# Expert 0's first rows built on TensorE from fp32 row tiles, with the experts' ranking and the splitting of weights in another order

## The chip, the cores and the metric

One core of a Trainium2 chip runs the whole block in one launch. The metric is the device time of one execution in microseconds (us), as the median of several runs. Engines are named as the profile names them: PE is TensorE's matrix product, PEld its weight load, DVE VectorE, ACT ScalarE, POOL GpSimd, SP the queue that issues most transfers.

## The reference

```python
hn = rms_norm(h, attn_norm_g[l])
u_raw, v_raw, q, k, v, gate_a, gate_b = split(hn @ w_in[l])
a = gmlp_chunk_mixer(u_raw, v_raw, ...)
b = swa_sink_attention(q, k, v, sinks, rel_bias)
merged = sigmoid(gate_a) * (a @ w_proj_a[l]) + sigmoid(gate_b) * (b @ w_proj_b[l])
h = h + merged @ w_out[l]
hn = rms_norm(h, ffn_norm_g[l])
# hierarchical MoE on hn: the best of 4 groups, in it the best 2 of 4 experts
for e in range(16):
    hid = silu(t @ w_gate[e]) * (t @ w_up[e])
    out = out + combine[:, e:e + 1] * (hid @ w_down[e])
h = h + out
return rms_norm(h, final_norm_g)
```

All is float32: 1024 tokens of 1024 channels, 16 experts with 512 hidden channels. A token goes to two experts, so an expert has about 128 tokens, some more and some fewer.

## The kernel before

Every large product is made of three fp32r products of a high part and a low part (`mm3`, lines 198 to 201): ACT writes the high part (a copy to fp32r), DVE subtracts it from the source and writes the low part. For weights this is done in "granules" of 128 x 1024 (`Granules`, from line 247): `high(g)` is an ACT instruction (line 299), `low(g)` a DVE instruction (line 305 for the gate and up weights, line 309 for the down weights), and `load_others(g)` then lets SP load a later granule into the raw buffer that became free. Expert e has the granules 12e to 12e+11: eight of gate and up (k = 0 to 7), four of down. In the tables of the change "h3" and "l3" are the high and the low part of granule 3 of the next expert.

The first part (norms, mixers, output projection) works on two halves of four 128-token tiles. In the second half the four tiles 4 to 7 leave the output projection one by one. For each `logits` makes the router's products and `route` chooses the experts, counts ranks within each expert on PE, and scatters the normalised rows (`row`, 1024 channels and a few words more) into the queues `xs_d` in DRAM by two indirect transfers on POOL. From the last tile on, DVE and ACT run in the order in which the code is written, and in the experts all engines do.

Expert 0 must begin while the rows of the last tiles are still on their way to `xs_d`. So its first 128 rows are put together in the core: the rows of tiles 0 to 5 are read back from `xs_d` into `early` (a DMA of POOL, line 1051), and the rows of tiles 6 and 7 (`LATE`) are placed by PE (`place`, line 1038): a 128 x 128 matrix of ones and zeros (`oh`, "place" in the profile) times the row tile, whose high and low parts (`hl`) come from ACT and POOL (line 1078). The sum lies in PSUM as rows; DVE adds it to `early` (line 1238), PE transposes the sum (eight transposes, `transpose_x`, line 1325), and ACT and DVE split it into `xT`. Then PE loads expert 0's count of tokens into a register, and branches: over 128 tokens it computes a second tile of the expert (`last_tile`), else it goes on. In the shown execution expert 0 has no second tile.

`order_experts` sorts the other experts by their counts (first part: ranks and row offsets; second part: counts and tables) in small DVE instructions, and writes them into `ints`. PE, ACT, DVE, POOL and SP read their branch conditions from there. The order of all this inside an expert's tile is set by `ahead(step)`: after a step such as ("f1", 7) or ("y", 1) of the matrix products it runs what the tables `AHEAD_0`, `AHEAD_1` and `AHEAD` name. `fill(k)` makes the expert's first two steps beside the second tile of the expert, with `FIRST` = 3 granules of the next expert in `fill(0)`.

## Time and profile before

| | us |
|---|---|
| median of 3 runs | 1094.59 |
| the three runs | 1091.77, 1094.59, 1094.70 |
| profiled execution | 1091.46 |
| its span | 1089.7 |
| PE busy in the span | 1023.1 (94%) |
| DVE busy | 724.8 (67%) |
| ACT busy | 608.7 (56%) |
| POOL busy | 107.6 (10%) |

The span runs from the first to the last profiled instruction; 1.8 us of the execution lie around it. In the profile a row of the timeline gives the start in us from the span's start, the time until the last instruction of the row ended, engine and line, what is written and read, how many instructions, and in brackets how long the engine had been idle and what ended that. Matrix products overlap: one of 512 columns is shown with 0.39 us, but they start 0.23 us after each other. A row with windows gives the busy time of each engine in a stretch, the granted clock of TensorE as a share of full speed, and the share of the DMA engines.

### The profile page before, as it was taken

The numbers are of one execution on the slowest core, as the hardware profiler recorded it, in microseconds if no ns is written. First come the engines' busy times: TensorE is split into PE (matmuls) and PEld (weight loads), VectorE is DVE, ScalarE is ACT, GpSimd is POOL, SyncE is SP. The second block draws the span as 40 slices with busy tenths as digits, with TensorE's granted clock in tenths as the row PEclk, the third lists the DMA queues.
The fourth block names the chain that finished last, engine by engine and source line by source line (L and its number), as shares of the span: only waits on it lengthen the run. The fifth ranks groups of instructions, "written<-read, shape, count | busy, mean of one in ns | idle before, by whom it ended". The sixth has DMA issues, their size and how long they took to land. (4 is left out here: it accounts for less than half of the span.)

```text
span 1089.7 us, 15458 instructions
## 1 busy us (share of the span) xinstructions
PE 1023.1 (94%) x4775; PEld 821.1 (75%) x4775; DVE 724.8 (67%) x1584; ACT 608.7 (56%) x1016; POOL 107.6 (10%) x132
## 2 busy tenths in 40 slices
PE   7999899999999999999999958899999999999893
PEld 6778788788888888887888846677777777777682
DVE  6852577675368555776445788978769686848735
ACT  5543465543356464555335447676858686847743
POOL 4001000000004000000001041111111112010020
PEclk9999999999999999999999989999999999999997
DMA  8432545645137413222646546969898989979854
GB/s 248 122 106 102 173 157 166 188 140 184 44 120 273 140 54 97 83 72 68 203 152 215 196 175 223 330 241 319 281 334 258 313 293 285 306 240 309 252 218 191
DMA packets 125478, 214.47 MB, mean 197 GB/s; under 512 B 11563, under 2 KB 58731, under 8 KB 125360
## 3 DMA queue, kind: packets, MB, share of 16 engines
q1 hardware_dynamic: 112016, 176.58, 48.6%
q0 software_dynamic: 7200, 21.20, 7.0%
q10 hardware_dynamic: 6144, 15.27, 3.8%
q8 instruction: 56, 0.92, 0.3%
q14 instruction: 62, 0.51, 0.1%
HBM read 185.46 MB, written 37.63 MB: 205 GB/s over the span
## 5 line engine op out<-in xcount | busy, mean ns | idle before, releaser
L305 DVE SCALAR_TENSOR_TENSOR w_e<-raw_e,g2T,w_e 128x1024 fp32r<-128x1024 f32 x127 | 156.1, 1280 | 22.9 <-ACT w_e L299 16.6
L299 ACT ACTIVATE w_e<-raw_e,g2T 128x1024 fp32r<-128x1024 f32 x127 | 137.5, 1142 | 15.1 <-DMA raw_e<-in_expert_w_up_dram 4.5
L199 PE MATMUL ps_gu<-w_e,xT 128*128 128x512 f32 x256 | 104.2, 407 | 8.9 <-ACT w_e L299 4.1
L201 PE MATMUL ps_gu<-w_e,xT 128*128 128x512 f32 x256 | 101.8, 398 | 1.1 <-DVE xT L177 1.1
L1413 PE MATMUL ps_y<-w_e,hT 128*128 128x512 f32 x384 | 100.4, 404 | 1.1 <-DVE hT L177 0.9
L200 PE MATMUL ps_gu<-w_e,xT 128*128 128x512 f32 x256 | 101.5, 396 | 0.0
L1413 PEld LDWEIGHTS ps_y<-w_e,hT 128*128 128x128 f32 x384 | 69.9, 190 | 17.3 <-DVE hT L177 1.8
L309 DVE TENSOR_TENSOR w_e<-raw_e,w_e 128x1024 fp32r<-128x1024 f32 x63 | 75.0, 1218 | 0.8 <-ACT w_e L299 0.8
L299 ACT ACTIVATE w_e<-raw_e 128x1024 fp32r<-128x1024 f32 x63 | 65.7, 1054 | 0.4 <-DMA raw_e<-in_expert_w_down_dram 0.2
L199 PEld LDWEIGHTS ps_gu<-w_e,xT 128*128 128x128 f32 x256 | 48.7, 190 | 20.7 <-issue 9.7
L201 PEld LDWEIGHTS ps_gu<-w_e,xT 128*128 128x128 f32 x256 | 48.8, 190 | 12.9 <-DVE xT L177 1.5
L200 PEld LDWEIGHTS ps_gu<-w_e,xT 128*128 128x128 f32 x256 | 48.8, 191 | 10.1
L201 PE MATMUL ps_o<-w_wo,ms 128*128 128x512 f32 x128 | 51.3, 402 | 0.0
L200 PE MATMUL ps_o<-w_wo,ms 128*128 128x512 f32 x128 | 51.1, 400 | 0.0
L199 PE MATMUL ps_o<-w_wo,ms 128*128 128x512 f32 x128 | 51.1, 399 | 0.0
L199 PE MATMUL ps_ga<-xh,w_ga 128*128 128x512 f32 x128 | 50.8, 397 | 0.0
L200 PE MATMUL ps_ga<-xh,w_ga 128*128 128x512 f32 x128 | 50.7, 396 | 0.0
L201 PE MATMUL ps_ga<-xh,w_ga 128*128 128x512 f32 x128 | 50.6, 396 | 0.0
L200 PE MATMUL ps_gb<-xh,w_gb 128*128 128x512 f32 x128 | 50.6, 395 | 0.0
L201 PE MATMUL ps_gb<-xh,w_gb 128*128 128x512 f32 x128 | 50.6, 395 | 0.0
L199 PE MATMUL ps_gb<-xh,w_gb 128*128 128x512 f32 x128 | 50.6, 395 | 0.0
L567 PE MATMUL ps_gv<-w_gv,xh 128*128 128x512 f32 x192 | 46.9, 397 | 3.9 <-ACT xh L176 2.5
(540 smaller groups left out, 2379.8 us busy)
## 6 DMA issues: line engine op xcount, KB each, us to landing
raw_e<-in_expert_w_gate_dram SPq DMA_DIRECT2D x127, 256.0 KB
raw_e<-in_expert_w_up_dram SPq DMA_DIRECT2D x127, 256.0 KB
raw_e<-in_expert_w_down_dram SPq DMA_DIRECT2D x63, 512.0 KB
xs_d<-zero ACTq DMA_DIRECT2D x16, 516.0 KB
xt_last<-xs_d SPq DMA_DIRECT2D x32, 258.0 KB
raw_ga<-in_w_in_dram SPq DMA_DIRECT2D x16, 512.0 KB
raw_gb<-in_w_in_dram SPq DMA_DIRECT2D x16, 512.0 KB
raw_wo<-in_w_out_dram SPq DMA_DIRECT2D x16, 512.0 KB
```

Of the source, the lines that this page charges most:

```text
L199: nc.tensor.matmul(acc, lhi, rhi, start=start, stop=False)
L200: nc.tensor.matmul(acc, lhi, rlo, start=False, stop=False)
L201: return nc.tensor.matmul(acc, llo, rhi, start=False, stop=stop)
L299: nc.scalar.activation(self.split_tiles[g][:, 0, :], self.raw[g], AF.Copy, **scale)
L305: nc.vector.scalar_tensor_tensor(w[:, 1, :], raw, g2T[:, k : k + 1], w[:, 0, :], ALU.mult, ALU.subtract)
L309: nc.vector.tensor_tensor(w[:, 1, :], raw, w[:, 0, :], ALU.subtract)
L567: nc.tensor.matmul(accs[i], xh[a][k // 4][:, k % 4, t], gs[j][:, b, k % 2, :], start=k + a + b == 0, stop=k == KT - 1 and b == 1,)
L1413: nc.tensor.matmul(ys[nh], hT[:, a, k, :], dn[k][:, b, nh * 512 : (nh + 1) * 512], start=k + i == 0, stop=k == FK - 1 and i == 2,)
```

## The change

- `LATE` takes in tile 5, so `early` holds tiles 0 to 4 and is read back before the scatters of tile 5.
- `place` no longer takes a high and a low part. The row tile is the stationary operand and the 128 x 128 one-hot matrix streams past it, both in plain fp32, in eight products of 128 columns for the eight blocks of channels. The result is already transposed. `early` is added in the same way with the identity as the one-hot matrix, as the last eight products. The `hl` tiles, ACT's and POOL's instructions for them, DVE's two additions and the eight transposes go.
- Tile 5's products stand around the transposes of tile 7's `logits`; tile 6's behind the logits; tile 7's and `early`'s at the end.
- High parts of granules 9, 10, 11 and 12 are issued on ACT within tile 7's routing; 20 warming transposes there become 10, and the 32 at the program's start become 42.
- Count and tables of expert 0 come ahead of `transpose_x`, the first part of `order_experts` right behind it, and the second part after ("y", 2) of expert 0 ahead of that step's low parts. Low parts of the next experts move to later steps (`AHEAD_0`, `AHEAD_1`), expert 1's `fill(0)` splits none, and one comparison (`at`) is made twice.
- Expert 0 has one form of a second tile left (a whole one), so it has one branch and less code in between.

```diff
-LATE = (6, 7)
+LATE = (5, 6, 7)
-AHEAD_0 = {("f1", 7): "h3 l3 h4 l4", ("y", 0): "h5 l5 h6 l6 h7 l7", ("y", 1): "h8 l8 h9 l9 h10 l10 h11 l11"}
+AHEAD_0 = {
+    ("f1", 5): "l0", ("f1", 7): "h3 l3", ("y", 0): "h4 l4",
+    ("y", 2): "h5 l5 h6 l6 h7 l7 h8 l8 h9 l9 h10 l10 h11 l11",
+}
-ORDER_AT = {("f1", 5), ("y", 2)}
+ORDER_AT = ("y", 2)
-WARM = 32
-WARM_ROUTE = 20
+WARM = 42
+WARM_ROUTE = 10
...
+                        place(*late[0], range(4), first=True)
+                        between = functools.partial(place, *late[0], range(4, KT), first=True)
...
-        def place(i, hl, oh):
+        def place(rows, oh, ks=range(KT), first=False, stop=False):
-            for nh in range(2):
-                cs = slice(nh * 512, (nh + 1) * 512)
-                for j in range(2):
-                    nc.tensor.matmul(
-                        xlate[nh], oh, hl[:, j, cs], start=(i + j == 0), stop=(i + j == len(LATE))
-                    )
+            for k in ks:
+                nc.tensor.matmul(
+                    xlate[k // 4][:, k % 4 * P : (k % 4 + 1) * P], rows[:, k * P : (k + 1) * P], oh,
+                    start=first and k % 4 == 0, stop=stop and k % 4 == 3,
+                )
...
-                        nc.gpsimd.tensor_tensor(hl[:, 1, cs], row[:, cs], hl[:, 0, cs], ALU.subtract)
...
-                    place(len(late) - 1, *late[-1])
+                    place(*late[-1])
+                    place(early[0][:, 0, :], ident, stop=True)
...
-        for nh in range(2):
-            cs = slice(nh * 512, (nh + 1) * 512)
-            nc.vector.tensor_tensor(xearly[0][:, cs], xlate[nh], xearly[0][:, cs], ALU.add)
...
-    xT, meta = transpose_x(xearly[0], "0", 2, xs_d[0:P, D:XW])
+    n = count_of(0)
+    hint("more0", n > P)
+    place_tables(slice(0, 2), ebase)
+    xT, meta = transpose_x(None, "0", 2, xs_d[0:P, D:XW], pts=xlate)
+    ordering = order_experts()
+    next(ordering)
...
-        first = range(12 * e + 12, 12 * e + 12 + (FIRST if e else 0))
+        first = range(12 * e + 12, 12 * e + 12 + (FIRST if e > 1 else 0))
```

PE, from the last tile's logits (`ps_l`) to the branch ahead of expert 0, before:

```order
L997 MATMUL ps_l_1_5811<-rw,hT_1_5809 128x20 x4
L1038 MATMUL ps_late_5851<-hl_5708,place_5711 128x512 x2
L1038 MATMUL ps_late_5852<-hl_5708,place_5711 128x512 x2
L207 MATMUL ps_warm<-ident 128x128 x20
...
L1134 MATMUL ps_cnt<-ecum,ones_b 128x16
L1038 MATMUL ps_late_5851<-hl_5879,place_5882 128x512 x2
L1038 MATMUL ps_late_5852<-hl_5879,place_5882 128x512 x2
L1325 MATMUL ps_xT_0_5988<-ident,early 128x128 x4
L1325 MATMUL ps_xT_1_5993<-ident,early 128x128 x4
L1446 TENSOR_LOAD ints
L1564 COMPARE_AND_BRANCH
```

and now:

```order
L1016 MATMUL ps_l_1_5831<-rw,hT_1_5829 128x20 x4
L1055 MATMUL ps_late_5812<-place_5723,row_5721 128x128 x4
L1055 MATMUL ps_late_5813<-place_5723,row_5721 128x128 x4
L215 MATMUL ps_warm<-ident 128x128 x10
...
L1146 MATMUL ps_cnt<-ecum,ones_b 128x16
L1055 MATMUL ps_late_5812<-place_5894,row_5892 128x128 x4
L1055 MATMUL ps_late_5813<-place_5894,row_5892 128x128 x4
L1055 MATMUL ps_late_5812<-ident,early 128x128 x4
L1055 MATMUL ps_late_5813<-ident,early 128x128 x4
L1465 TENSOR_LOAD ints
L1591 COMPARE_AND_BRANCH
```

Behind the last count stand sixteen products of 128 columns in place of four of 512 and eight transposes; the load of the count and the branch follow as before.

POOL, from the scatters (`xs_d<-row`) of tile 4 to those of tile 7, before:

```order
L1200 DMA xs_d<-row_5420,si_5484 16384x1032 x2
L1079 COPY row_5707<-ids 128x1
L1080 MEMSET row_5707 128x3
L1200 DMA xs_d<-row_5563,si_5627 16384x1032 x2
L1078 TENSOR_TENSOR hl_5708<-row_5707,hl_5708 128x512 x2
L1051 DMA early<-xs_d 128x1024
L1079 COPY row_5878<-ids 128x1
L1080 MEMSET row_5878 128x3
L1078 TENSOR_TENSOR hl_5879<-row_5878,hl_5879 128x512 x2
L1200 DMA xs_d<-row_5707,si_5821 16384x1032 x2
L1200 DMA xs_d<-row_5878,si_5955 16384x1032 x2
```

and now:

```order
L1217 DMA xs_d<-row_5430,si_5494 16384x1032 x2
L1068 DMA early<-xs_d 128x1024
L1089 COPY row_5721<-ids 128x1
L1090 MEMSET row_5721 128x3
L1217 DMA xs_d<-row_5574,si_5641 16384x1032 x2
L1217 DMA xs_d<-row_5721,si_5843 16384x1032
L1089 COPY row_5892<-ids 128x1
L1090 MEMSET row_5892 128x3
L1217 DMA xs_d<-row_5721,si_5843 16384x1032
L1217 DMA xs_d<-row_5892,si_5971 16384x1032 x2
```

POOL's two pairs of subtractions are gone, and the read of `early` stands ahead of tile 5's scatters.

DVE, at the end of expert 0, from the split of expert 1's rows (`xT`) on; L309 are low parts of down weights, the rows from `big` on the second part of the ranking; before:

```order
L177 TENSOR_TENSOR xT_5985<-ps_xT_0_6493,xT_5985 128x512
L177 TENSOR_TENSOR xT_5985<-ps_xT_1_6498,xT_5985 128x512
L309 TENSOR_TENSOR w_e_5376<-raw_e_6056,w_e_5376 128x1024
L309 TENSOR_TENSOR w_e_5525<-raw_e_6061,w_e_5525 128x1024
L309 TENSOR_TENSOR w_e_5668<-raw_e_6066,w_e_5668 128x1024
L309 TENSOR_TENSOR w_e_5669<-raw_e_6071,w_e_5669 128x1024
L1273 TENSOR_TENSOR big<-at,cnt 128x256
L1274 TENSOR_REDUCE cnt<-big 128x16
L1275 CAST ints<-cnt 128x14
```

and now:

```order
L185 TENSOR_TENSOR xT_6043<-ps_xT_0_6371,xT_6043 128x512
L185 TENSOR_TENSOR xT_6043<-ps_xT_1_6376,xT_6043 128x512
L1282 TENSOR_TENSOR at<-el_rank,rank_at 128x256
L1292 TENSOR_TENSOR big_6391<-at,cnt 128x256
L1293 TENSOR_REDUCE cnt<-big_6391 128x16
L1294 CAST ints<-cnt 128x14
...
L1323 CAST ints<-far_6413 128x14
L313 SCALAR_TENSOR_TENSOR w_e_5264<-raw_e_5389,g2T,w_e_5264 128x1024
L313 SCALAR_TENSOR_TENSOR w_e_5310<-raw_e_5392,g2T,w_e_5310 128x1024
```

The ranking moved ahead of the low parts, of which seven now follow it; before, four of them stood ahead of it and three had gone before the split of the rows.

## Rows read from the trace of the kernel before

**Rows 1.** Windows: busy us of PE, PEld, DVE, ACT, POOL; clock, DMA share, GB/s.
```profile
640.00:660.00 20.00, 11.93 (x54) 9.38 (x53) 16.99 (x53) 9.68 (x14) 7.30 (x7) 0.74 0.36 135
700.00:800.00 100.00, 96.62 (x443) 75.89 (x442) 77.94 (x109) 72.61 (x99) 15.64 (x12) 1.00 0.88 291
```

**Rows 2.** Timeline of PE, from the last output projection to expert 0's first product.
```profile
630.89 0.40 PE L201 MATMUL ps_o<-w_wo,ms 128*128 128x512 f32 x1
...
635.64 0.18 PE L1128 MATMUL ps_r<-eb,up_b 128*128 128x16 bf16 x1 [2.84 <-DVE eb L1125]
...
636.93 2.05 PE L1038 MATMUL ps_late<-hl,place 128*128 128x512 f32 x4
...
643.99 0.18 PE L1128 MATMUL ps_r<-eb,up_b 128*128 128x16 bf16 x1 [2.43 <-DVE eb L1125]
...
644.93 1.18 PE L1038 MATMUL ps_late<-hl,place 128*128 128x512 f32 x4 [0.69 <-DVE sp L1178]
646.92 1.97 PE L1325 MATMUL ps_xT<-ident,early 128*128 128x128 f32 x8 [0.81 <-DVE early L1238]
653.03 0.76 PE L199 MATMUL ps_gu<-w_e,xT 128*128 128x512 f32 x1 [4.15 <-ACT w_e L299]
```

**Rows 3.** Timeline of DVE and POOL in the routing of tiles 6 and 7.
```profile
631.11 0.16 DVE L1149 TENSOR_TENSOR dv<-v,v 128x4 f32<-128x4 f32 x1
...
632.20 2.96 DVE L1029 TENSOR_TENSOR oh<-ft_b,fr_b 128x16 f32<-128x16 f32 x1
632.62 2.50 POOL L1078 TENSOR_TENSOR hl<-row,hl 128x512 fp32r<-128x512 f32 x2
...
640.69 1.24 DVE L1149 TENSOR_TENSOR dv<-v,v 128x4 f32<-128x4 f32 x1
...
641.96 1.20 DVE L1150 TENSOR_TENSOR dv<-dv,goh 128x4 f32<-128x4 f32 x1
...
644.44 0.34 DVE L1172 TENSOR_SCALAR place<-islot,rk,mine 128x128 fp32r<-128x128 bf16 x1
```

**Rows 4.** Timeline of PE: an fp32 product of 384 columns, and eight transposes.
```profile
76.86 0.81 PE L428 MATMUL ps_bias<-bias,rb 32*8 32x384 f32 x2
...
669.39 1.03 PE L1325 MATMUL ps_xT<-ident,xt_first 128*128 128x128 f32 x8
```

**Rows 5.** Windows of 2 us, columns as in rows 1: TensorE's granted clock.
```profile
636.00:638.00 2.00, 2.00 (x10) 1.81 (x10) 1.96 (x18) 0.00 (x0) 0.33 (x3) 0.56 0.59 168
...
644.00:646.00 2.00, 1.31 (x8) 0.82 (x8) 1.59 (x13) 0.00 (x0) 1.32 (x2) 1.00 0.56 231
```

**Rows 6.** Timeline of POOL: tile 5's second scatter and the read of `early`.
```profile
631.64 0.96 POOL L1200 DMA_INDIRECT xs_d<-row,si  x1 [0.30 <-PE ps_o L201]
...
635.50 0.60 POOL L1051 DMA_DIRECT2D early<-xs_d  x1 [0.38 <-DMA xs_d<-row,si]
```

**Rows 7.** Timeline of DVE and PE in experts 0, 1 and the start of 2.
```profile
663.69 0.42 DVE L1369 TENSOR_TENSOR hid<-hid,ps_gu 128x256 f32<-128x256 f32 x1 [2.33 <-ACT hid L1368]
664.03 0.17 DVE L1259 SCALAR_TENSOR_TENSOR rk_key<-cnt,misc 128x16 f32<-128x16 f32 x1
...
666.74 0.42 DVE L177 TENSOR_TENSOR hT<-ps_hT,hT 128x256 fp32r<-128x256 f32 x1
...
670.46 3.67 DVE L305 SCALAR_TENSOR_TENSOR w_e<-raw_e,g2T,w_e 128x1024 fp32r<-128x1024 f32 x3
...
681.55 0.47 PE L199 MATMUL ps_gu<-w_e,xT 128*128 128x512 f32 x1 [2.78 <-DVE ints L1278]
...
701.22 0.28 DVE L177 TENSOR_TENSOR xT_last<-ps_xT_2h,xT_last 128x128 fp32r<-128x128 f32 x1
```

**Rows 8.** Windows, columns as in rows 1, of experts 0 to 2.
```profile
663.70:701.20 37.50, 30.93 (x145) 23.01 (x143) 35.92 (x62) 27.95 (x37) 3.84 (x3) 1.00 0.85 288
```

**Rows 9.** Timeline of PE at the program's start.
```profile
2.07 6.67 PE L207 MATMUL ps_warm<-ident 128*128 128x128 f32 x32 [2.07 <-POOL ident masks.py:199]
10.34 1.09 PE L541 MATMUL ps_x<-ident,xn 128*128 128x128 f32 x8 [1.60 <-DVE xn L535]
```

More of the change, by code (lines that the diff above doesn't have):

```diff
@@ L984, in setup_moe, with logits @@
             nc.sync.dma_start(rank_at, c_misc[32:48].partition_broadcast(P))
-        def logits(n, nh, h, ssq):
+        def logits(n, nh, h, ssq, between=None):
             junk = tmp2(f"junk_{n}_{nh}")
@@ L992, in logits @@
                 nc.tensor.transpose(pt[:, k * P : (k + 1) * P], h[:, k * P : (k + 1) * P], ident)
+            if between:
+                between()
             hT = tmp2(f"hT_{n}_{nh}")
@@ L1059, in route @@
             if n == LATE[-1]:
-                for i, parts in enumerate(late):
-                    place(i, *parts)
+                place(*late[1])
                 keep_warm(ps_mm, WARM_ROUTE)
@@ L1068, in route @@
                 rows.append(row)
-                if n + i in LATE:
-                    hl = slot8([P, 2, D], F32R, f"hl_{n + i}")
-                    nc.scalar.activation(hl[:, 0, :], h, AF.Copy, scale=r)
                 nc.scalar.activation(row[:, 0:D], h, AF.Copy, scale=r)
                 if n + i in LATE:
-                    oh = moe.tile([P, 256], F32, tag="hid", name=f"place_{n}")[:, 0:P].bitcast(F32R)
-                    late.append((hl, oh))
-                    for nh in range(2):
-                        cs = slice(nh * 512, (nh + 1) * 512)
-                        nc.gpsimd.tensor_tensor(hl[:, 1, cs], row[:, cs], hl[:, 0, cs], ALU.subtract)
+                    oh = moe.tile([P, 256], F32, tag="hid", name=f"place_{n}")[:, 0:P]
+                    late.append((row, oh))
                 nc.gpsimd.tensor_copy(row[:, D + 4 : D + 5].bitcast(I32), ids[:, n + i : n + i + 1])
                 nc.gpsimd.memset(row[:, D + 5 : XW], 0.0)
+            if n == LATE[-1]:
+                granules.high(10)
             l = small_tile([T, 20], "l", n)
@@ L1146, in weights @@
                 nc.scalar.activation(ge, ge, AF.Exp)
+                if n == LATE[-1]:
+                    granules.high(11)
                 expert_onehot(0, oh1)
@@ L1235 @@
         nc.vector.tensor_copy(cnt_i[:, 0:2], pc[:, 0:2])
-        for nh in range(2):
-            cs = slice(nh * 512, (nh + 1) * 512)
-            nc.vector.tensor_tensor(xearly[0][:, cs], xlate[nh], xearly[0][:, cs], ALU.add)
     def order_experts():
@@ L1310, in load_x, with transpose_x @@
         return xt
-    def transpose_x(xt, name, first=4, meta_src=None, xT=None):
+    def transpose_x(xt, name, first=4, meta_src=None, xT=None, pts=None):
         if xT is None:
@@ L1320, in transpose_x @@
             nc.sync.dma_start(meta, meta_src)
-        pts = []
-        for q in range(2):
+        pts = pts or []
+        for q in range(len(pts), 2):
             pt = ps_tp(f"ps_xT_{name}_{q}")
@@ L1455, in last_rows @@
         nc.sync.dma_start(xt[H:P], xs_d[bass.ds(start + H, H), :], cond=n > P)
-        both = n > (P if e == NE - 1 else P + H)
+        both = n > (P if e in WHOLE else P + H)
         nc.sync.dma_start(xt[0:H], xs_d[bass.ds(start, H), :], cond=both)
@@ L1562, in beside, with whole_tile @@
                 fill(1)
+        def whole_tile():
+            xl, ml = transpose_x(xlast, f"{e}l", 4, None, xT)
+            fill(0)
+            expert_tile(xl, ml, e, dup_i[:, e : e + 1], f"{e}l", beside, **banks)
         with tc.If(n > P, label=f"more{e}") as more:
-            with tc.If(n <= P + H) as few:
-                half_tile(xlast, xT, mlast, e, f"{e}h", fill)
-            with few.Else():
-                xl, ml = transpose_x(xlast, f"{e}l", 4, None, xT)
-                fill(0)
-                expert_tile(xl, ml, e, dup_i[:, e : e + 1], f"{e}l", beside, **banks)
+            if e in WHOLE:
+                whole_tile()
+            else:
+                with tc.If(n <= P + H) as few:
+                    half_tile(xlast, xT, mlast, e, f"{e}h", fill)
+                with few.Else():
+                    whole_tile()
         with more.Else():
@@ L1661 @@
     xT_last = slot8([P, 2, KT, P], F32R, "xT_last")
-    xT, meta = transpose_x(xearly[0], "0", 2, xs_d[0:P, D:XW])
+    n = count_of(0)
[4 more added lines that the diff above has]
+    next(ordering)
     granules.low(7)
     granules.load_others(7)
-    place_tables(slice(0, 2), ebase)
     xnext = first_rows(1)
-    n, *lasts = last_rows(0)
-    hint("more0", n > P)
-    for g in range(9, 15):
-        granules.split(g)
+    n, *lasts = last_rows(0, n)
+    for g in (13, 14):
+        granules.high(g)
+    for g in (9, 10, 11, 13, 14):
+        granules.low(g)
+        granules.load_others(g)
     nc.scalar.activation(one, one, AF.Silu)
-    ordering = order_experts()
     for e in range(NE - 1):
```

46 lines of the change are left out of this document (30 added, 16 removed).

## The prediction

> **What bounds the kernel now.** I read the windows of the whole span first. In the experts PE is busy 96.6 of 100 us; the one stretch before them in which no engine is full is 640 to 660, where PE has 11.9 of 20 us [rows 1]. That is the passage from the last routed tile to expert 0. Then I read PE's timeline there, and asked of each gap who ended it. The last output projection starts at 630.89, and expert 0's first product at 653.03 [rows 2]: 22 us in which PE does little but wait. The gaps: 2.84 us for `eb` of tile 6, 2.43 us for `eb` of tile 7, 0.69 and 0.81 us for the one-hot matrix and for `early`, and 4.15 us ahead of the first expert product [rows 2]. The first four are DVE's chain of small instructions.
>
> Third, that chain. A small DVE instruction takes 0.16 us here. Three take far longer: 2.96, 1.24 and 1.20 us [rows 3]. The first ends at 635.16, as POOL's pair of subtractions, 2.50 us from 632.62, ends [rows 3]; the other two lie beside POOL's second pair. So DVE stands while POOL subtracts, and the chain is late by (2.96 - 0.16) + (1.24 - 0.16) + (1.20 - 0.16) = 4.9 us.
>
> Last, what takes over once PE starts earlier. From expert 0's first `hid` (663.69) to the split of expert 2's second tile (701.22) DVE is busy 35.9 of 37.5 us [rows 7, 8], PE 30.9. There DVE is the bound, and a gain on PE alone is worth nothing.
>
> **The change, part by part.**
>
> *POOL's subtractions go.* Gain 4.9 us on DVE's chain, all of it on the path: `eb` of both tiles and the one-hot matrix of tile 7, which starts at 644.44 [rows 3], move up by it, to 639.5. ACT loses its two `hl` copies too; they don't set the end.
>
> *The last products.* Before, PE needs from 644.93 to 646.92 + 1.97 = 648.89: 3.96 us for four products, two additions on DVE and eight transposes [rows 2]. Now sixteen fp32 products of 128 columns start at 644.93 - 4.9 = 640.0. No such product is in the trace. The nearest is the fp32 product of 384 columns: it appears as two instructions, both in 0.81 us [rows 4]. If each is shown with the fixed tail of about 0.17 us that a 512-column product has over its pitch (0.39 against 0.23), a pass costs 0.32 us for 384 columns, 0.11 for 128. Eight transposes, also one pass of 128 columns with a weight load each, take 1.03 us, 0.12 each at full clock [rows 4]. So I take 32 passes of 0.12 plus the tail: 4.0 us, PE done at 644.0, no gain and no loss against 3.96. Upper bound: the pace of the transposes at 646.92, 1.97 us for eight, 0.24 a pass at the lower clock [rows 2]: 7.8 us. Below the transposes' pace nothing in the trace goes; no gain is assumed. I stay at the low end since the products have the shape of the transposes at 669.39, and since PE is kept busy ahead of them: after a gap of 2.84 us the granted clock was 0.56 over 2 us, so partly at 1.2 GHz, and four placing products took 2.05 us; after one of 2.43 us it was still 1.00 (2.4 GHz) and they took 1.18 [rows 2, 5]. The new gaps (from the end of the ten warming transposes to 640) come to about 2.2 us.
>
> A rule speaks against that. The Trainium skill, FP8 and Floating Point Precision, TensorE Precision Notes, says that true fp32 makes four passes through the array. The trace's two instructions at 0.32 us for 384 columns agree if each holds two passes of one column a cycle; were it four passes of a transpose's length, it is the first rival below.
>
> *Tile 5's and 6's products.* Eight products of two passes each, 1.9 us a tile. Four of tile 5's fill the wait for DVE's addition ahead of the logits, the rest and tile 6's fall into the old gap of 2.84 us and the place of tile 6's 2.05 us and ten transposes [rows 2]. Cost nothing; without that cover 0.5 us.
>
> *The gap ahead of expert 0* (4.15 us, [rows 2]) is put down to ACT, but the high part that the product needs is written long before. On PE stand only the load of the count and the branch, now as before behind the last product. I keep the 4.15. First expert product: 644.0 + 4.15 = 648.2, with rounding 648.5 against 653.03, a gain of 4.5. DVE's tables, the split of `xT` and the first part of the ranking lie in this gap and behind it, ahead of anything expert 0 waits for.
>
> *Experts 0 and 1.* `hid` of expert 0 moves with PE: 663.69 - 4.5 = 659.2. From there DVE sets the pace. Out of its work goes the first part of the ranking, 664.03 to 666.74, 2.7 us [rows 7]. In come one low part (1.2 us, a third of 3.67, [rows 7]) and the second `at`, about 0.45. Saved 1.05. But low parts now come only after their high parts on ACT (three waits; a high part takes about as long as a low part, and I estimate 1.5 us for the three) and nothing else fills them. Net cost 0.3 to 0.5. The gap of 2.78 us in which PE waits for `ints` [rows 7] goes, since the ranking stands ahead of seven low parts; but those seven, 8.2 us, are then ahead of `hid` of expert 1, and PE waits there, and again for the split at 701.22. So that gap's 2.78 us are not a gain: the same DVE work must be done before expert 2. The split of expert 2's second tile then lies at 697.0, and PE's timeline from there on is the old one, moved by 4.2 us.
>
> *The added waits.* Tile 5's scatters wait for the read of `early` (their rows may not be there when it reads), and ACT's row tile 7, which reuses tile 5's buffer, waits for these scatters. Tile 5's second scatter was issued at 631.64 and had landed by 635.50, in 3.9 us [rows 6]; moved by the early read some 0.5 us, it lands at 636, when ACT wants the buffer. Behind it on ACT stand the row, a high part, the exponentials, and DVE's `gsum` waits for the first of them. Cost 0, at most the lateness of the landing. SP's order keeps the loads that the low parts release; the rows of expert 2 are asked for as late as before.
>
> *Ten more warming transposes at the start.* 10 x 0.21 = 2.1 us against 1.60 us of idle time behind them [rows 9]: at most 0.5 us, and there DVE and loads are late anyway. I take 0. *One branch less, one form less*: expert 0 takes neither form. 0.
>
> **Sum.** 4.9 (POOL) + 0 (last products) - 0.4 (rounding at the start) - 0.3 (DVE in experts 0 and 1) = 4.2 us. From the profiled 1091.46 us that is 1087.3; from the median, 1094.59, it is 1090.4. The four executions lie at 1091.5 to 1091.8 and 1094.6 to 1094.7, so the median stands 3.1 above the profile without a cause that I can name. I predict from their middle, 1093.1: 1088.9 us.
>
> **The rivals.** (a) *The products take longer*: four passes of 0.12 a product, or two at the lower clock. 16 x 4 x 0.12 = 7.7 us, PE done at 647.8, expert 0 at 652.0, gain 1.0 less 0.3. For it: no such row, the clock falls around here [rows 5]. Against it: the 384-column row. 1093.1 - 0.7 = 1092.4. (b) *The gap of 4.15 us shrinks*, because less code is jumped over. Then PE could begin as soon as `xT` is split, and DVE would set the pace: the split of `xT` ends at an estimated 645.7, the ranking (2.7 us) and six low parts (7.2 us) at 655.6, so `hid` starts there and not at 659.2: 3.5 us more, 1085.4. For it: nothing that the product reads is late in that gap. Against: the branch stays, right behind the load. The Trainium skill, Runtime: NRT & Kernel Launch, Instruction fetch mechanics, holds that a taken branch to code not yet fetched stalls the engine; that fits the gap, and leaves open whether a shorter jump is spared it. (c) *Slower*: the passes don't overlap with their weight loads and run at the lower clock, 2 x 0.24 = 0.48 less what a load shares, say 0.43 each. 32 x 0.43 = 13.8 us, expert 0 at 640.0 + 13.8 + 4.15 = 658.0, 5.0 us late: 1093.1 + 5.3 = 1098.4. It decides from a pass of (653.03 - 4.15 - 640.0) / 32 = 0.28 us on. Against it: even at the lower clock eight transposes took 0.24 each. (d) *DVE isn't freed*: if the three long instructions waited for something other than POOL, the 4.9 us stay, and with the rest even the time is the old one, 1093.
>
> **How the numbers follow.** Forecast 0.52, (a) 0.22, (b) 0.13, (c) 0.07, (d) 0.06. About 0.3% (3.3 us) is what a measurement of this kernel can tell from no change. The forecast's 4.2 us is close above that, and I count a fifth of it as less; so faster 0.42 + 0.13 and a little of (a) = 0.57; within 0.3%: 0.10 + most of (a) + (d) and a part of (c) = 0.34; slower 0.09. The range goes from (b) at 1085 to (a) and no change at the upper level of the runs, 1094: 1084.8 to 1094.0. Below lies a tenth, above (c).
>
> **What would show it.** In the profile after: no small DVE instruction over 0.5 us in tiles 6 and 7; the last sixteen products as 32 instructions in 4 us at a clock of 1.00 (over 7 us: rival a); about 4 us between them and expert 0's first product (under 2: rival b); PE waiting for `hid` of expert 1 and for the split of expert 2's second tile, and no longer for `ints`; that split some 4 us earlier. I am wrong if PE's first expert product is not 3 to 6 us earlier, or if it is and the split at 701.22 is not.

## The result and the profile after

The changed kernel takes 1101.2 us (median of six runs), the kernel before, run beside it on the same chip, 1094.5. The ratio is 1.006, with a 95% interval of 1.004 to 1.008: **slower by 0.6%**. Five of the six runs lie between 1098.8 and 1103.3; the sixth took 1439.5 us at a granted clock of 0.65, and it is in the median, which without it is 1100.0, but not in the ratio. I had forecast 1088.9 and faster. The profiled execution took 1100.0 us with a span of 1098.3, that of before 1091.46 with 1089.7.

First, where the 8.6 us between the two spans lie. I cut PE's timeline at the last output projection (`ps_o`), expert 0's first product, and the first transposes of experts 1 and 2:

| stage, us | before | after | difference |
|---|---|---|---|
| start to the last `ps_o` | 630.9 | 632.2 | +1.3 |
| last `ps_o` to expert 0's first product | 22.1 | 17.1 | -5.0 |
| expert 0 | 16.4 | 18.6 | +2.3 |
| expert 1 | 24.6 | 26.2 | +1.6 |
| experts 2 to 14 | 337.2 | 345.3 | +8.2 |
| expert 15 and the end | 58.5 | 58.8 | +0.3 |

The second stage, which I call the passage, is what the change aims at, and it became shorter. All of that and more was lost behind it. The profile after, by engine, in the passage (timelines; columns as before):

```profile
635.67 2.03 PE L1055 MATMUL ps_late<-place,row 128*128 128x128 f32 x16
...
642.91 0.19 PE L1140 MATMUL ps_r<-eb,up_b 128*128 128x16 bf16 x1 [4.11 <-DVE eb L1137]
...
643.87 3.75 PE L1055 MATMUL ps_late<-place,row 128*128 128x128 f32 x16 [0.69 <-DVE sp L1195]
647.41 2.12 PE L1055 MATMUL ps_late<-ident,early 128*128 128x128 f32 x16
649.29 0.48 PE L207 MATMUL ps_gu<-w_e,xT 128*128 128x512 f32 x1
...
629.16 0.59 POOL L1068 DMA_DIRECT2D early<-xs_d  x1 [3.49 <-issue]
...
633.71 1.00 POOL L1217 DMA_INDIRECT xs_d<-row,si  x1 [3.73 <-DVE e L1165]
635.02 0.96 POOL L1217 DMA_INDIRECT xs_d<-row,si  x1 [0.30 <-issue]
...
640.18 1.15 ACT L1085 ACTIVATE row<-h,rstd 128x1024 f32<-128x1024 f32 x1 [3.51 <-DMA xs_d<-row,si]
...
639.51 0.15 DVE L1164 TENSOR_TENSOR dv<-dv,goh 128x4 f32<-128x4 f32 x1
...
642.40 0.16 DVE L1171 TENSOR_REDUCE gsum<-ge 128x1 f32<-128x4 f32 x1 [2.40 <-ACT ge L1158]
```

These rows answer to [rows 2, 3, 6]. DVE's small instructions are back at 0.15 us, as forecast. But the read of `early` now stands ahead of tile 5's scatters on POOL, and the first of these goes out only at 633.71, after 3.73 us; the second at 635.02. The row names DVE's `e`, which belongs to tile 6; in a3 (below) it names another instruction of tile 6, and the wait is the same. What fits both is the read's own landing (transfers of POOL's queue, KB and us from issue to landing):

```profile
early<-xs_d POOLq DMA_DIRECT2D x1, 512.0 KB, 3.7
```

Until the second scatter has landed ACT can't write row tile 7, and waits 3.51 us, to 640.18. Behind that row and a high part stands the exponential; `gsum` on DVE waits 2.40 us for it, and PE 4.11 us for `eb`. After that idle time the eight products of `place` for tile 7 (sixteen records) ran at half clock (windows; columns as in [rows 1]):

```profile
643.00:647.00 4.00, 3.31 (x19) 3.25 (x20) 2.73 (x20) 1.45 (x3) 0.96 (x1) 0.50 0.19 76
...
660.00:680.00 20.00, 18.10 (x79) 14.89 (x80) 16.46 (x34) 12.76 (x17) 2.04 (x1) 0.91 0.52 169
...
680.00:700.00 20.00, 13.78 (x57) 9.99 (x55) 17.15 (x21) 13.87 (x18) 4.47 (x2) 0.83 1.02 325
```

and the same view of the kernel before, for the last two stretches:

```profile
660.00:680.00 20.00, 17.62 (x81) 13.40 (x79) 17.23 (x29) 14.50 (x20) 1.69 (x1) 1.00 0.75 259
680.00:700.00 20.00, 16.05 (x77) 12.19 (x78) 18.86 (x35) 13.51 (x19) 1.88 (x2) 1.00 0.96 317
```

The granted clock was 0.50 (1.2 GHz) in 643 to 647. From 660 to 680 the DMA engines moved 169 GB/s, before 259; from 680 to 700 they are full in both kernels, and PE is busy 13.8 us instead of 16.1. In these two stretches PE was granted 0.91 and 0.83, before 1.00. Behind that stand these rows of experts 0 to 2 (timelines, as [rows 7]; SPq is SP's queue of transfers, DVEq DVE's sequencer):

```profile
651.07 0.16 DVE L1272 SCALAR_TENSOR_TENSOR rk_key<-cnt,misc 128x16 f32<-128x16 f32 x1
...
659.58 1.28 DVE L313 SCALAR_TENSOR_TENSOR w_e<-early,g2T,w_e 128x1024 fp32r<-128x1024 f32 x1
661.42 0.42 DVE L1389 TENSOR_TENSOR hid<-hid,ps_gu 128x256 f32<-128x256 f32 x1 [0.57 <-ACT hid L1388]
...
661.01 0.38 ACT L1388 ACTIVATE hid<-ps_gu 128x256 f32<-128x256 f32 x1 [6.99 <-DVEq L1591]
...
657.40 0.40 PE L209 MATMUL ps_gu<-w_e,xT 128*128 128x512 f32 x1
...
661.90 0.69 PE L1395 MATMUL ps_hT<-ident,hid 128*128 128x128 f32 x2 [2.71 <-DVE hid L1389]
662.81 0.63 PE L208 MATMUL ps_gu<-w_e,xT 128*128 128x512 f32 x1
...
670.57 0.42 DVE L1282 TENSOR_TENSOR at<-el_rank,rank_at 128x256 f32<-128x256 f32 x1
674.57 3.67 DVE L313 SCALAR_TENSOR_TENSOR w_e<-raw_e,g2T,w_e 128x1024 fp32r<-128x1024 f32 x3
...
670.02 0.33 SPq L288 DMA_DIRECT2D raw_e<-in_expert_w_up_dram  x1
675.88 0.33 SPq L288 DMA_DIRECT2D raw_e<-in_expert_w_gate_dram  x1
...
683.79 0.33 SPq L1328 DMA_DIRECT2D xt_first<-xs_d  x1
...
683.83 0.44 PE L1395 MATMUL ps_hT<-ident,hid 128*128 128x128 f32 x2 [2.46 <-DVE hid L1389]
694.13 1.09 PE L1344 MATMUL ps_xT<-ident,xt_first 128*128 128x128 f32 x8 [3.75 <-DMA xt_first<-xs_d]
694.98 4.60 PE L1433 MATMUL ps_y<-w_e,hT 128*128 128x512 f32 x12
703.06 1.19 PE L1513 MATMUL ps_gu_2h<-w_e,xT_last 128*128 128x512 f32 x4 [1.26 <-DVE xT_last L185]
```

The ranking's second part holds DVE from 670.57 to 674.57, and the low parts that release raw buffers come behind it. SP's loads pause from 670.02 to 675.88, and expert 2's rows are asked for at 683.79, behind these loads, 3.1 us later than before (680.70). They land when PE has waited 3.75 us for them. The product at 657.40 is the 36th of expert 0, the last that ACT's `hid` needs.

### The profile page after: what moved, and what is told of

It is laid out like the page before. It is cut to its first block, busy times and chain, and to the rows that moved or that the text cites. A ratio compares the mean times of both kernels' runs of the same rounds, so it can differ in the third digit from the quotient of the medians.

```text
span 1098.3 us, 15559 instructions
## 1 busy us (share of the span) xinstructions
PE 1029.1 (94%) x4823; PEld 828.0 (75%) x4823; DVE 719.9 (66%) x1585; ACT 606.9 (55%) x1014; POOL 102.3 (9%) x128
## 5 line engine op out<-in xcount | busy, mean ns | idle before, releaser
L307 ACT ACTIVATE w_e<-raw_e,g2T 128x1024 fp32r<-128x1024 f32 x127 | 138.0, 1143 | 17.1 <-PE ps_gu L209 5.5
L1433 PE MATMUL ps_y<-w_e,hT 128*128 128x512 f32 x384 | 102.7, 412 | 0.4 <-ACT hT L184 0.4
```

What stands on the lines that cost most here:

```text
L307: nc.scalar.activation(self.split_tiles[g][:, 0, :], self.raw[g], AF.Copy, **scale)
L1433: nc.tensor.matmul(ys[nh], hT[:, a, k, :], dn[k][:, b, nh * 512 : (nh + 1) * 512], start=k + i == 0, stop=k == FK - 1 and i == 2,)
```

## The experiments

Kernels whose labels begin with the same letter ran beside each other and beside the kernel before on one chip (its median there was 1093.5 to 1094.5). Stages are those of the table above, from one profiled execution each.

| kernel | passage | expert 0 | expert 1 | experts 2 to 14 | median | ratio to before, 95% |
|---|---|---|---|---|---|---|
| before | 22.1 | 16.4 | 24.6 | 337.2 | 1094.5 | |
| after | 17.1 | 18.6 | 26.2 | 345.3 | 1101.2 | 1.006 (1.004 to 1.008) |
| a1 | 18.4 | 18.4 | 25.6 | 340.5 | 1094.7 | 1.000 (0.998 to 1.002) |
| a2 | 12.7 | 19.4 | 26.3 | 347.4 | 1099.2 | 1.004 (1.002 to 1.006) |
| a3 | 16.9 | 16.3 | 25.9 | 343.4 | 1094.9 | 1.001 (1.000 to 1.003) |
| a4 | 16.9 | 18.5 | 25.1 | 346.2 | 1101.6 | 1.007 (1.005 to 1.009) |
| b1 | 14.1 | 16.3 | 25.8 | 337.8 | 1087.9 | 0.995 (0.993 to 0.997) |
| b2 | 16.9 | 16.3 | 25.9 | 345.1 | 1098.9 | 1.004 (1.002 to 1.006) |
| b3 | 17.0 | 20.9 | 25.4 | 346.5 | 1099.2 | 1.004 (1.003 to 1.006) |
| b4 | 16.4 | 17.4 | 26.1 | 343.4 | 1093.7 | 0.999 (0.997 to 1.001) |
| c0 (as b1) | 13.5 | 20.3 | 25.3 | 340.4 | 1092.6 | 0.998 (0.996 to 1.001) |
| c1 | 16.7 | 16.3 | 25.8 | 340.2 | 1093.0 | 1.000 (0.997 to 1.002) |
| c2 | 14.1 | 17.4 | 27.0 | 342.4 | 1094.5 | 1.001 (0.999 to 1.003) |
| c3 | 14.1 | 17.4 | 27.1 | 340.9 | 1092.8 | 1.000 (0.997 to 1.002) |
| d0 (as b1) | 12.7 | 17.1 | 25.8 | 338.2 | 1089.9 | 0.996 (0.994 to 0.998) |
| d1 | 22.0 | 16.0 | 26.4 | 338.7 | 1097.9 | 1.003 (1.002 to 1.005) |
| d2 | 17.0 | 18.6 | 22.3 | 349.2 | 1098.8 | 1.006 (1.004 to 1.008) |
| d3 | 16.8 | 18.6 | 22.6 | 345.9 | 1095.5 | 1.002 (1.000 to 1.004) |

Single executions lie up to 3 to 6 us from their kernel's median, one 9 us, so a stage of one execution proves little by itself; verdicts rest on medians and means of six to twelve runs (five for the mean of after), and on waits that stand in every trace of a kind. The ratios are of means. Two kernels of one letter can be told apart when their means differ by some 2 to 2.5 us; a difference with a plus-minus below is one of means, with its 95% uncertainty.

**a1: one last form for expert 0, on the kernel before.**

```diff
-            with tc.If(n <= P + H) as few:
-                half_tile(xlast, xT, mlast, e, f"{e}h", fill)
-            with few.Else():
-                xl, ml = transpose_x(xlast, f"{e}l", 4, None, xT)
...
+            if e == 0:
+                whole_tile()
```

> The kernel before, with one thing of the change alone: expert 0's last tile has one form in the code instead of two, so the jump past it is shorter. Nothing of the computation changes. Theory: the 4.15 us in which the tensor engine stands ahead of expert 0 is the price of that jump (in the changed kernel it is gone); it falls under 1 us, and the whole is some 4 us shorter than the kernel before, ratio 0.996, or less if the transfers give some of it back. Rival: the gap went because the count of expert 0 is read earlier in the changed kernel, or because of the order of the ScalarE parts; then the gap stays at about 4 us here and the ratio is 1.000.

Timeline of PE in a1, expert 0's first product and the transpose of its first `hid`:

```profile
649.78 0.76 PE L199 MATMUL ps_gu<-w_e,xT 128*128 128x512 f32 x1 [0.40 <-issue]
...
662.90 0.44 PE L1375 MATMUL ps_hT<-ident,hid 128*128 128x128 f32 x2 [1.38 <-DVE hid L1369]
```

The gap of 4.15 us [rows 2] is 0.40: it came with the second form that PE jumps over. The Trainium skill, Runtime: NRT & Kernel Launch, Instruction fetch mechanics, states that a taken branch whose target isn't among the pages already fetched stalls the engine until its page is loaded; the gap agrees with that in kind, but no run here shows the loading itself. The time stayed: 1094.7, 0.1 ± 1.4 us over the kernel before. The first product is 3.3 us earlier, but `hid` is ready only 1.2 us earlier (the transpose that waits for it starts at 662.90; before, `hid` ended at 663.69 + 0.42, [rows 7]), and PE waits for it.

**a2: the early read behind tile 5's scatters again**, tile 5 with them; the rest as after.

```diff
-LATE = (5, 6, 7)
+LATE = (6, 7)
...
-                place(*late[1])
+                place(*late[0], first=True)
```

> The changed kernel, with the early read of the first 128 rows put back behind tile 5's two scatters (only tiles 6 and 7 are placed by products, in fp32). Theory: ScalarE's row_7 waits 3.51 us in the changed kernel because tile 5's scatters stand behind the early read; with them in front again row_7 starts at its rstd, VectorE's wait of 2.40 us for the exponential goes, the tensor engine's wait for eb falls from 4.11 to about 1.7 us and the 16 products of tile 7 that took 3.75 us at half clock take about 2 us: 3 to 5 us less than the changed kernel, some 1096 to 1098 (ratio to before 1.002). Rival: the wait only moves to the early read itself, which lands later; then the time stays at 1101 (ratio 1.006).

Timelines of ACT and PE in a2:

```profile
635.53 1.15 ACT L1081 ACTIVATE row<-h,rstd 128x1024 f32<-128x1024 f32 x1
...
638.99 0.18 PE L1136 MATMUL ps_r<-eb,up_b 128*128 128x16 bf16 x1 [1.48 <-DVE eb L1133]
...
639.94 2.02 PE L1051 MATMUL ps_late<-place,row 128*128 128x128 f32 x16 [0.69 <-DVE sp L1191]
...
656.95 0.69 PE L1391 MATMUL ps_hT<-ident,hid 128*128 128x128 f32 x2 [2.87 <-DVE hid L1385]
```

ACT no longer waits for the row's buffer, PE waits 1.48 us instead of 4.11, and the sixteen products run at full pace, 2.02 us. Expert 0's first product comes 12.7 us behind the last `ps_o` instead of 17.1. That is worth about 2 us (1.9 ± 2.1 against a4, and the interval overlaps after's). So tile 5's new place costs some 2 us, at the edge of what can be told; with a passage 9.4 us shorter than in the kernel before, a2 is still slower than it.

**a3: the old order of ranking and low parts**; the rest as after. **b2 and b3** put back one half of that each: b2 the ranking's places alone, b3 the low parts' places alone.

```diff
-ORDER_AT = ("y", 2)
+ORDER_AT = {("f1", 5), ("y", 2)}
...
-    next(ordering)
...
-    for g in (9, 10, 11, 13, 14):
+    for g in range(9, 15):
...
-        first = range(12 * e + 12, 12 * e + 12 + (FIRST if e > 1 else 0))
+        first = range(12 * e + 12, 12 * e + 12 + (FIRST if e else 0))
```

(and `AHEAD_0`, `AHEAD_1` as before; b2 has the first two edits, b3 the others.)

> The changed kernel, with the experts' order and the low parts of expert 1's and 2's weights where the kernel before has them (the order's first half in expert 0's gate and up, its second half at expert 0's last product; the low parts in the old places). Theory: the 2.71 us wait for expert 0's hid and the 6 us in which SyncE's loads stand (669.5 to 675.9) come from that order; with it undone SyncE issues the 16 loads without a break, expert 2's rows arrive in time (the wait of 3.75 us goes), and the whole is 5 to 9 us shorter than the changed kernel: 1092 to 1096, ratio to before 1.000. Rival: those waits are only the share of a late start of the routing, and come back elsewhere: 1099 to 1101, ratio 1.005.

> The changed kernel with the two halves of the experts' order alone put back (first half at step f1,5 of expert 0, second half at its last product as now); the low parts stay in the new places. Theory: it is the first half (2.8 us of VectorE) ahead of the low parts of granules 9 to 14 that makes expert 0's hid 2.71 us late and drops the clock after it; this gives 2 to 4 us, 1097 to 1099 us, ratio 1.003. Rival: the low parts' places alone are the cost, then this is as the changed kernel, ratio 1.006.

> The changed kernel with the low parts of experts 0, 1 and 2 alone in their old places; the order's first half stays ahead of them. Theory: the loads of expert 2's weights then follow one another without the break from 669.5 to 675.9 us, expert 2's rows come in time (the wait of 3.75 us goes): 3 to 5 us less than the changed kernel, ratio 1.002. Rival: the order's first half is the whole cost; then ratio 1.006, and the two together (1.001 in the run that undid both) come from it.

Timeline of POOL in a3, tile 5's first scatter:

```profile
634.24 1.00 POOL L1212 DMA_INDIRECT xs_d<-row,si  x1 [3.78 <-DVE eb L1132]
```

The early read is still ahead of it there. a3 is 5.6 ± 1.8 us under a4, 6.7 by medians, and 5.5 under after's mean: this order is where most of the loss of 6.6 us lies. Either half alone brings about 2 us (ratio 1.004 in b2 and b3), no more than the uncertainty. Their traces show that the halves cost by different waits; PE in b2, expert 2's rows, and in b3, expert 0's first `hid`:

```profile
689.40 1.37 PE L1344 MATMUL ps_xT<-ident,xt_first 128*128 128x128 f32 x8 [3.60 <-DMA xt_first<-xs_d]
...
661.98 0.69 PE L1390 MATMUL ps_hT<-ident,hid 128*128 128x128 f32 x2 [3.90 <-DVE hid L1384]
```

With the low parts in the new places (b2) the rows are late; with the ranking ahead of the low parts (b3) `hid` is. At 675 us DVE had finished 9 low parts in after, 12 in before, 16 in b1.

**a4: 32 warming transposes at the start** instead of 42 (`WARM = 32`).

> The changed kernel with 32 warming products at the start instead of 42. Theory: the 1.27 us that the changed kernel is late already at 35 us (16 ps_gv products in 5.44 us where the kernel before takes 3.95) come with the 42; then this is 1.3 us shorter than the changed kernel, ratio to before 1.005, and the products take 3.95 us. Rival: that dip comes and goes from run to run or comes from another instruction order in the first stage; then no difference, ratio 1.006.

1101.6 against 1101.2 (0.1 ± 2.3 by means): no effect that can be told from none, and the 1.3 us of this run's theory lie within that. In a4's trace the dip is gone (sixteen `ps_gv` products in 3.95 us, in after 5.44), but the last `ps_o` starts only 0.2 us earlier than in after (631.92 against 632.16).

**b1, c0, d0: a2, a3 and a4 together**, one kernel, measured three times on three chips. It keeps of the change the fp32 products for tiles 6 and 7, the one form, and the high parts in the routing.

> The changed kernel with three parts undone at once: the early read behind tile 5's scatters (tiles 6 and 7 alone placed by products), the experts' order and the low parts in their old places, 32 warming products. What stays of the change: the fp32 products, one last form for expert 0, the ScalarE parts of granules 9 to 12 inside the routing. If the two costs add (2.0 us for the early read, 6.3 us for the order, as the runs that undo each alone gave), this takes 1093 us, ratio 0.998 to 0.999. Rival: expert 0 starts some 9 us earlier than in the kernel before (643 instead of 653 us), but experts 0 to 2 wait for VectorE and for transfers that set the pace anyway; then the start is given back and the time is that of the kernel before, ratio 1.000 to 1.002. If nothing of the start were given back it would be 9 us faster, ratio 0.992.

> The combination again, unchanged, as the anchor of the three that follow on the same chip. Expected as measured: 1087.9 us, ratio 0.995; if it was luck of that chip, 0.998 or more.

> The combination (fp32 products for tiles 6 and 7, one last form for expert 0, the order and the low parts in their old places) a third time, as the anchor of this call and because its two results differ (ratios 0.9949 and 0.9984). Expected between them: 1088 to 1092.5 us, ratio 0.995 to 0.9985. If it is 0.9985 or more, the combination is no faster than the kernel before by what can be measured.

Ratios 0.995, 0.998 and 0.996, mean 0.9965: about 3.8 us faster than before, 10 faster than after, though one of three intervals reaches 1. Its passage is 8.0 to 9.5 us shorter. Expert 0 took 16.3, 20.3 and 17.1 us in the same code. Timeline of PE, the transpose of expert 0's first `hid` and the products behind, in c0:

```profile
656.61 0.69 PE L1386 MATMUL ps_hT<-ident,hid 128*128 128x128 f32 x2 [3.06 <-DVE hid L1380]
...
657.52 0.63 PE L203 MATMUL ps_gu<-w_e,xT 128*128 128x512 f32 x1
```

and in d0:

```profile
657.66 0.44 PE L1386 MATMUL ps_hT<-ident,hid 128*128 128x128 f32 x2 [1.34 <-DVE hid L1380]
...
658.18 0.40 PE L203 MATMUL ps_gu<-w_e,xT 128*128 128x512 f32 x1
```

The last `ps_o` was 2.9 us earlier in c0 than in d0 (630.16 against 633.08), and PE came to the transpose 2.8 us earlier, but `hid` only 1.05. So PE waited 3.06 us there instead of 1.34, and went on with products of 0.63 us instead of 0.40: the granted clock was 0.50 in 657 to 659, in d0 1.00 in 658 to 660. The earlier start became a wait, and a lower clock followed.

**b4: the products alone**, as b1 with two forms for expert 0 and the high parts 9 to 12 behind the routing; **c3** the high parts alone behind it, with the one form.

```diff
-WHOLE = 0, NE - 1
+WHOLE = (NE - 1,)
...
-                        granules.high(9)
...
-            if n == LATE[-1]:
-                granules.high(10)
```

(c3 lacks the first edit.)

> The combination above without the two other parts that were left in it: expert 0 has two last forms again and the ScalarE parts of granules 9 to 12 stand behind the routing as before. What stays is the placing of tiles 6 and 7 by fp32 products with the transposed result. Theory: the routing's last tile ends some 5 us earlier than before (no subtractions on GpSimd beside VectorE, no sum, no transposes), but the 4 us gap ahead of expert 0 is there again: expert 0 starts at 648 to 649 us. If the start is worth what it moves, 4 us less than before, ratio 0.996; if experts 0 to 2 give it back, 1.000.

> The combination with the ScalarE parts of granules 9 to 12 behind the routing again, as in the kernel before; expert 0 keeps one last form. Beside the run without both (1093.7 us, a gap of 3.5 us ahead of expert 0) this tells which of the two made the combination 5.8 us faster. Theory: the one form, since it takes the gap away: 1088 to 1090, ratio 0.995 to 0.996. Rival: the ScalarE parts, since low parts 9 to 12 on VectorE wait for them and expert 0's hid stands behind these: then 1092 to 1094, although the gap is gone, as in the kernel before with one form alone (1094.7).

Timeline of PE in b4, expert 0's first product:

```profile
648.77 0.76 PE L202 MATMUL ps_gu<-w_e,xT 128*128 128x512 f32 x1 [3.48 <-ACT w_e L302]
```

With two forms the gap is back, 3.48 us; in c3, with one, PE waits 1.12 us there for `xT`. b4 is 4.5 ± 2.4 us over b1 (5.8 by medians), so the one form and the high parts together seem to be worth something there. But c3, without the high parts, is only 0.6 ± 2.4 us over c0, and beside the kernel before b4 and c3 hardly differ (ratios 0.999 and 1.000, on two chips). Which of the two it is, and whether b1's six runs were merely lucky, stays open.

**c1: a delay of known size in the passage**, four additions of 128 x 512 on DVE ahead of tile 7's sum, on b1.

```diff
+                if n == LATE[-1]:
+                    for j in range(4):
+                        pad = tmp2(f"pad_{j}")
+                        nc.vector.tensor_tensor(pad, hs[0][:, 0:512], hs[0][:, 512:1024], ALU.add)
```

> The combination with four additions of 128x512 (nothing reads them), some 2.5 us of VectorE, put in front of the sum of the last tile's exponentials, at the place where VectorE stands 2.40 us when the early read is ahead of tile 5's scatters. Theory: a stall of the last tile's chain is paid once, with the half clock that follows it: 2.5 to 4 us longer than the combination, 1090.5 to 1092, ratio 0.997 to 0.998. Rival: a later start of expert 0 is given back or is multiplied by transfers behind it: then 1088 (hidden) or 1095, as with the early read ahead (7 us).

The additions take 2.5 us, the passage is 2.5 to 3.2 us longer than b1's and c0's, and the median 0.4 above c0's (0.7 ± 2.5). A price of one for one is at the upper end of that, so it is unlikely but not excluded.

**c2: the loads' pause alone**, on b1: a store of 2 KB that reads granule 21's split holds SP's queue, and the loads of granules 17 to 20 go behind it.

```diff
-                    granules.load_others(g)
+                    if e or g < 17:
+                        granules.load_others(g)
+                    if e == 0 and g == 21:
+                        nc.sync.dma_start(...)
+                        for late_g in range(17, 21):
+                            granules.load_others(late_g)
```

> The combination with nothing but its weight loads delayed: in expert 0, after the first two of the loads that follow expert 1's low parts, SyncE's queue waits for the low part of expert 1's tenth granule (a store of 2 KB that reads it), so that the other loads and expert 2's rows start some 6 us later, as in the changed kernel; the order of VectorE and ScalarE is untouched. Theory: the changed kernel's later low parts cost mainly through these late loads (expert 2's rows are waited for 3.75 us there): 3 to 6 us longer than the combination, 1091 to 1094. Rival: the loads have slack, and the cost is VectorE's order itself (expert 0's and 1's hid late): then within 1 us of the combination.

The first of these loads goes out at 671.77, in b1 at 665.98 and in c0 at 665.59, so some 6 us late. Expert 2's rows are asked for at 681.92, in c0 at 674.37, and PE still doesn't wait for them. The median is 1.8 us over c0's, the mean 2.3 ± 1.9: the pause of the loads by itself may cost some 2 us, and it isn't the whole of the order's loss.

**d1: the new order on the kernel before**, nothing else (a3's edit the other way round).

> The kernel before, with one part of the change alone: the first half of the experts' order ahead of the low parts of granules 9 to 14, its second half at expert 0's last product, and the low parts of experts 0 to 2 in the changed places. Theory: this part costs the kernel what undoing it gave the changed kernel, some 6 us: 1100 us, ratio 1.005 to 1.006, wherever expert 0 starts. Rival: in the kernel before the 4 us gap ahead of expert 0 leaves VectorE time for the order's first half, so it costs only what the late loads cost: 1095 to 1097, ratio 1.002.

Timeline of PE in d1: expert 0's first product, and the transposes of expert 2's rows.

```profile
652.16 0.76 PE L204 MATMUL ps_gu<-w_e,xT 128*128 128x512 f32 x1 [4.03 <-ACT w_e L304]
...
694.60 1.97 PE L1335 MATMUL ps_xT<-ident,xt_first 128*128 128x128 f32 x8 [4.72 <-DMA xt_first<-xs_d]
```

The order alone costs 3.9 us (1097.9 against 1094.0). In the jump's gap of 4.03 us, up to 652.16, DVE does the ranking's first part (649.70 to 652.41), and expert 0 takes 16.0 us; but PE waits 4.72 us for expert 2's rows.

**d2: these rows asked for earlier**, on after.

```diff
+                if e == 0:
+                    got["next"] = first_rows(2)
...
-            if step == ("y", 2) and e + 2 < NE:
+            if step == ("y", 2) and 0 < e < NE - 2:
```

> The changed kernel with the read of expert 2's first rows put in front of the loads that wait for the low parts of expert 1's granules 5 to 11 (it needs only the order's first half, which the changed kernel has early). Theory: the 3.75 us wait for these rows and the half clock after it go: 3 to 5 us less than the changed kernel, 1096.5 to 1098.5, ratio 1.003. Rival: the wait is only where a delay shows that VectorE or the loads set anyway (expert 1's hid, expert 2's weights); then 1100 to 1102, ratio 1.006.

**d3: after without expert 1's low parts of granules 17 to 23** (`if not 17 <= g < 24` ahead of `granules.low(g)`). The kernel leaves these parts out, so its products use what the buffers held before.

> The changed kernel without VectorE's low parts of expert 1's granules 5 to 11 (left out, not moved: 8.3 us of VectorE; the products run over old data, and the loads behind them wait for ScalarE alone). Theory: VectorE sets the pace of experts 0 and 1 and holds the loads back; without these parts expert 1's hid and expert 2's rows come in time and 5 to 8 us go: 1093 to 1096, ratio 1.000. Rival: what the changed kernel loses is lost later, to transfers and to the start of code, whatever VectorE does here: 1099 to 1101, ratio 1.005.

Timeline of PE in d2, two waits of experts 1 and 2:

```profile
682.16 0.44 PE L1395 MATMUL ps_hT<-ident,hid 128*128 128x128 f32 x2 [2.46 <-DVE hid L1389]
...
699.66 0.51 PE L1513 MATMUL ps_gu_2h<-w_e,xT_last 128*128 128x512 f32 x1 [4.04 <-DVE xT_last L185]
```

and in d3:

```profile
679.23 0.38 PE L1395 MATMUL ps_hT<-ident,hid 128*128 128x128 f32 x2
...
688.54 1.97 PE L1344 MATMUL ps_xT<-ident,xt_first 128*128 128x128 f32 x8 [3.80 <-DMA xt_first<-xs_d]
```

In d2 the 3.75 us for the rows are gone, and PE waits 4.04 us for DVE's split instead of 1.26: no gain (ratio 1.006, as after). In d3 PE still waits for the rows, 3.80 us, yet it doesn't wait for `hid` of expert 1, and the time is 4.5 ± 2.2 us under d2's, 3.3 by medians. So in the order's loss DVE's work sets the pace rather than the late rows. d3 doesn't tell DVE's time from the loads that a missing low part releases sooner (they go without the pause there); by c2, on another kernel, the loads' pause is some 2 us.

## Why the prediction was wrong

**Right.** *POOL's subtractions*: in a2, where nothing else is in the way, `eb` of tile 7 comes 8.2 us behind the last `ps_o` (630.8), before 13.1: 4.9 us, the term as forecast. *A product's size*: sixteen records in 2.02 us at full pace (a2; 2.03 for tile 6 of after), 0.12 each, two to a product. Rival (a), a product as long as four transposes, is thereby out. The Trainium skill, FP8 and Floating Point Precision, TensorE Precision Notes, says only that true fp32 makes four passes; how many of them a record holds no run shows. The products of tiles 5 and 6 cost nothing (PE waits 4.11 us behind them), the warming transposes nothing that can be told (a4), and PE no longer waits for `ints`.

**"The added waits ... Cost 0, at most the lateness of the landing."** The first step that failed. I counted the read's issue, some 0.5 us, ahead of tile 5's scatters, and had the second land at 636. The scatter waits for the read to *land*, 3.73 us, then the scatters' own landing, at 640.2. `gsum`'s wait of 2.40 us took half of the 4.9 us; `eb` came 10.75 us behind the last `ps_o`. In time it is about 2 us (a2).

**"I stay at the low end"** for the last products. They took 3.75 + 2.12 less overlap, 5.4 us (643.87 to 649.29), against the 4.0 forecast: after a wait of 4.11 us PE was granted half clock. The wait I reckoned with was 2.2. My upper bound, 7.8, held it. In b1 even a wait of 1.49 us was followed by 3.47 us for sixteen records, in a2 one of 1.48 by 2.02: the length of the wait doesn't decide it alone.

**"I keep the 4.15."** Rival (b)'s mechanism was the true one: with a single form the gap is gone (a1, b4). Together with the two misses the first expert product came 3.7 us earlier, where I said 4.5: nearly right by errors that cancel. But (b)'s price, 3.5 us, was wrong too: a1 is worth nothing that can be measured. The gap had been cover for DVE. Without it PE reaches the transpose of expert 0's `hid` at 659.2. ACT's part of `hid`, whose last product ends at 657.80, starts only at 661.01: its row names DVE's sequencer at the branch (L1591), which stands behind a low part that ends at 660.86. I had seen that DVE sets the pace from `hid` on, but then moved `hid` with PE (659.2; it came at 661.42).

**"Net cost 0.3 to 0.5"** for experts 0 and 1, with the rows of expert 2 "asked for as late as before". This is the step that turned the sign. Undoing the order brings 5.6 ± 1.8 us (a3 against a4), doing it alone costs 3.9 (d1). I summed DVE's instructions, which did fall (2.7 us out, 1.65 in), and estimated 1.5 us for waits; I didn't follow what the moved order releases. It puts 2.7 us of ranking ahead of the first low parts, where the gap no longer hides it, and 4.0 us ahead of the rest: 9 low parts instead of 12 by 675 us, a pause of 5.9 us in the loads behind them, the rows 3.1 us late, PE waiting 2.71, 2.46, 3.75 and 1.26 us in turn, and products at half clock behind such waits (`ps_y`, twelve in 4.60 us). The split that I put at 697.0 came at 702.72, before 701.22.

**"PE's timeline from there on is the old one."** It lost 7.1 us more: from the split to the end of the span 395.6 us against 388.5. Waits of PE after, from 700 to 1040 (total us, times, longest):

```profile
PE ps_hT L1395 <- DVE hid L1389: 12.6, 11, 5.2
PE ps_gu L207 <- issue: 2.1, 1, 2.1
PE ps_xT_12l L1344 <- DMA xt_last<-xs_d: 1.9, 1, 1.9
PE ps_xT_6h L1494 <- DMA xt_last<-xs_d: 1.6, 1, 1.6
```

All waits there come to 21.3 us, before to 14.9; those for `hid` were 11.0, those for `xt_last` 1.2 instead of 4.9. With the old order experts 2 to 14 took 337 to 343 us in ten traces (before and a1 among them), with the new one, or a half of it, on the changed kernel 345 to 349 in seven. Yet d1 has the new order and took 338.7. So on the changed kernel the new order costs something behind expert 1 too, and **what carries it there stays open**: the rows above say where PE stood, not why. Part of the 7.1 may be the execution: the profiled run of before lies 3 us under its median, as the prediction said.

The rule of the prediction's last part, wrong if the first product is 3 to 6 us earlier "and the split at 701.22 is not", is what happened: 3.74 us earlier at the first product, 1.50 later at the split. Rival (c), the only slower one, gave 1098.4, near the time that came, but by luck: its products at 0.43 a pass would have taken 13.8 us, and they took 5.4.

## What to carry to other kernels

An earlier start is worth only what the engine behind it can use: the passage got 8 to 9.5 us shorter in b1, c0 and d0 for some 4 us, and 3.7 us shorter in a1 for nothing; so ask of each gap which other engine works in it. When instructions are reordered on an engine, follow what now stands later in its queue (here `hid`, the splits, and the low parts that release loads and the reads behind them), not the sum of the instructions: here the sum fell by 1 us and the time rose. And a scatter that must not pass a read waited here, as far as the rows tell, for the read's landing, 3.7 us, not for its issue.

## What the runs showed of the hardware

- A branch that jumped over two forms of the second tile cost PE 3.48 to 4.15 us (before, b4, d1), over one form at most 0.57 where no data was waited for (0.40 in a1, 0.57 in c0, none in after).
- Behind a branch that was jumped ACT's instruction waited until DVE, too, was past its work ahead of the branch: 3.2 us in after, from 657.80, when its input was ready, to 661.01 (the row's 6.99 us count ACT's whole idle time).
- The clock that PE gets behind the same wait differs from run to run of the same code: behind 1.50 and 1.49 us the same sixteen records took 2.02 us in c0, at a clock of 1.00, and 3.47 in b1, mostly at 0.50.
- One 128-column fp32 product stands in two records, about 0.25 us together at full clock (sixteen records in 2.02 in a2) and 0.43 to 0.47 at half (3.47 in b1, 3.75 in after).
